# Absolute values and the key factor of a gated linear recurrence: from VectorE to ScalarE

## The chip, the cores and the metric

The kernel runs on one core of one Trainium2 chip. The metric is device time in microseconds (us) of one execution; of several runs the median is given. The engines are TensorE (PE in the profile, PEld for its weight loads), VectorE (DVE), ScalarE (ACT), GpSimd (POOL) and SyncE (SP, which issues the DMAs).

## The reference

One step of a two-layer decoder over 1056 positions: a prompt of 1024 and 8 x 4 sample positions. The first layer is a gated linear recurrence (HGRN2) of 8 heads with a 128x128 state, the second an attention with dilated windows; each has a squared-ReLU MLP. The change lies in the gates of the recurrence:

```python
q, f, i, og = jnp.split((xn @ w_in).astype(jnp.float32), 4, axis=-1)
q = heads(jax.nn.silu(q), A_KDIM)
log_f = heads(jax.nn.log_sigmoid(f) + jnp.log1p(lb * jnp.exp(jnp.minimum(-f, EXP_CLAMP))), A_KDIM)
k = heads((1.0 - lb) * jax.nn.sigmoid(-f), A_KDIM)
v = heads(i, A_VDIM)
...
o = _head_rmsnorm(o, out_gain.reshape(A_HEADS, A_VDIM)) * heads(jax.nn.sigmoid(og), A_VDIM)
```

## The kernel before, in words

`phase_a` (from L326) computes the recurrence. The channels of one head lie on the 128 partitions, the 1056 positions on the free axis, cut into three chunks of 352. For each of the 8 heads four projections of the normed input are made on TensorE (f, q, the value i, and the output gate og of the head before), each as 8 x 3 matmuls per chunk, since every fp32 factor is split into a high and a low part (`mm3`, L185 to L187).

A projected chunk is copied out of PSUM by ScalarE (`ev_to`, L368; for f in `ev_f`, L390). Then the gates follow, chunk by chunk:

- `sigmoid` (L371) is called for q (as silu) and for og. It forms -|x| on VectorE (L376), then exp (L377) and ln(1 + .) (L378) on ScalarE, min(x, 0) minus that on VectorE (L380), exp on ScalarE (L381), and for q a product on VectorE (L383).
- `ev_f` forms -|f| on VectorE (L392), exp (L393) and ln(1 + .) (L394) on ScalarE, the log-sigmoid (L395) and the softplus (L396) on VectorE, the key exp(-softplus) on ScalarE (L397), its factor 1 - lb on VectorE (L398), then the second logarithm (L399 to L402) and the running sum along the positions on VectorE (L404, L408, L412).

The lower bound lb and 1 - lb are made once, from 8 columns (L336 to L341); the tile `e` holds them.

`gla` works the recurrence of one head off, in pieces: it is a generator, and after every half of a projection's chunk (`tick`, called in `mm3` where `fine` is set) the next piece is emitted between the projections' matmuls. One half of a head has seven levels of scores. A level is a subtraction on GpSimd (L536), two exponentials on ScalarE (L539, L540), two products on VectorE (L541, L543), matmuls on TensorE (L554) and a masked copy of their result into the tile `A` on VectorE (L558). Then come the decays (L566 to L573), the transposes of the decayed keys (L618 uses them), four states `S`, one from the other, on VectorE (L626, L628), and matmuls with A and S (L633, L635). The result is normed and gated on VectorE (L640, L647). `gla_sample` does the same for the sample positions.

Each engine works its instructions off in the order of its own queue. That order is fixed when the kernel is built: a planner walks through the program with its own estimates of durations and takes, on each engine, the ready instruction of the highest priority; priority is the order of the program, moved forward where `high_priority` says so (copies out of PSUM by 300, states by 200, levels by 50). A matmul that waits for a PSUM bank, for A or for S holds up every matmul behind it. Of the tiles of the change, `sg` has two buffers and `fn` one.

Of the kernel before, what the change touches and what calls it, by code (L numbers as in the profile page):

```python
# [13 lines left out]
AF = mybir.ActivationFunctionType  # L14
ALU = mybir.AluOpType
# [31 lines left out]
class Kern:  # L47
# [278 lines left out]
    def phase_a(self):  # L326
        nc, tc, a = self.nc, self.tc, self.a
# [7 lines left out]
        e = c.tile([P, 3, KD], F32, name="lbt")  # L335
# [3 lines left out]
        nc.vector.tensor_tensor(e[:, 0], e[:, 0], e[:, 1], op=ALU.mult)  # L339
        nc.vector.tensor_tensor(e[:, 1], e[:, 0], e[:, 0], op=ALU.subtract)  # L340
        nc.vector.tensor_scalar(e[:, 2], e[:, 1], -1.0, 1.0, op0=ALU.mult, op1=ALU.add)  # L341
        self.lb, self.omlb = e[:, 1], e[:, 2]
        ctx = ExitStack()
        s1 = ctx.enter_context(tc.tile_pool(name="gla1", bufs=1, reuse_waits="tile"))
        gp = self.gp = ctx.enter_context(tc.tile_pool(name="gla", bufs=2, reuse_waits="tile"))
# [25 lines left out]
        def sigmoid(x, mul):  # L371

            for c in range(NCH):
                x_ = x[:, c * CW:(c + 1) * CW]
                n = gp.tile([P, CW], F32, name="sg")
                nc.vector.scalar_tensor_tensor(n, x_, -1.0, x_, op0=ALU.mult, op1=ALU.min)  # L376
                nc.scalar.activation(n, n, AF.Exp)  # L377
                nc.scalar.activation(n, n, AF.Ln, bias=1.0)  # L378
                o = n if mul else x_
                nc.vector.scalar_tensor_tensor(o, x_, 0.0, n, op0=ALU.min, op1=ALU.subtract)  # L380
                nc.scalar.activation(o, o, AF.Exp)  # L381
                if mul:
                    nc.vector.tensor_tensor(x_, x_, n, op=ALU.mult)  # L383

        def ev_f(h, b, kt, lf):
            def ev(c, ps):
                sl = slice(c * CW, (c + 1) * CW)
                with hp():
                    f = gp.tile([P, CW], F32, name="fr")
                    nc.scalar.activation(f, ps, AF.Copy)  # L390
                n = gp.tile([P, CW], F32, name="fn", bufs=1)
                nc.vector.scalar_tensor_tensor(n, f, -1.0, f, op0=ALU.mult, op1=ALU.min)  # L392
                nc.scalar.activation(n, n, AF.Exp)  # L393
                nc.scalar.activation(n, n, AF.Ln, bias=1.0)  # L394
                nc.vector.scalar_tensor_tensor(lf[:, sl], f, 0.0, n, op0=ALU.min, op1=ALU.subtract)  # L395
                nc.vector.scalar_tensor_tensor(n, f, 0.0, n, op0=ALU.max, op1=ALU.add)  # L396
                nc.scalar.activation(kt[:, sl], n, AF.Exp, scale=-1.0)  # L397
                nc.vector.tensor_scalar(kt[:, sl], kt[:, sl], self.omlb[:, h:h + 1], None, op0=ALU.mult)  # L398
                nc.vector.tensor_scalar(f, f, -80.0, None, op0=ALU.max)  # L399
                nc.scalar.activation(f, f, AF.Exp, scale=-1.0)  # L400
                nc.scalar.activation(f, f, AF.Ln, scale=self.lb[:, h:h + 1], bias=1.0)
                nc.vector.tensor_tensor(lf[:, sl], lf[:, sl], f, op=ALU.add)  # L402
                n, off = min(CW, NP_ - c * CW), c * CW % P
                nc.vector.tensor_tensor_scan(  # L404
                    b[:, c * CW:c * CW + n], self.reset[:, off:off + n], lf[:, c * CW:c * CW + n],
                    0.0 if c == 0 else b[:, c * CW - 1:c * CW], op0=ALU.mult, op1=ALU.add)
                if n < CW:
                    nc.vector.tensor_tensor_scan(b[:, NP_:], self.reset[:, 448:], lf[:, NP_:], 0.0, op0=ALU.mult, op1=ALU.add)  # L408

                for i in ((), (2, 3), (6, 7))[c]:  # L410
                    s = slice(i * P, i * P + P)
                    nc.vector.scalar_tensor_tensor(b[:, s], lf[:, s], b[:, s.stop - 1:s.stop], b[:, s], op0=ALU.add, op1=ALU.subtract)  # L412
            return ev

        def gate(h, og):
            self.proj(self.wnext(), ops, ev_to(og))
            sigmoid(og, False)
            nc.gpsimd.tensor_copy(self.so[:, h, :], og[:, NP_:])

        self.fine = True  # L420
        for h in range(8):
            b = gp.tile([P, NT], F32, name="b")
            kt = gp.tile([P, NT], F32, name="k")
            q = gp.tile([P, NT], F32, name="q")
            lf = gp.tile([P, NT], F32, name="lf", bufs=1)
            if h == 0:
                w = [self.wnext(), self.wnext()]
                self.proj_n(w, ops, [ev_f(h, b, kt, lf), ev_to(q)])
                for i in range(4):
                    mt = gp.tile([P, 512], F32, name="lv", bufs=6)[:, :480]  # L430
                    nc.sync.dma_start(mt, a["masks"][:, 480 * i:480 * i + 480])
                    nc.vector.tensor_copy(self.masks[:, 480 * i:480 * i + 480], mt)
            else:
                gate(h - 1, og)
                self.proj(self.wnext(), ops, ev_f(h, b, kt, lf))
                self.proj(self.wnext(), ops, ev_to(q))
            sigmoid(q, True)
            vT = gp.tile([P, NT], F32, name="vT", bufs=1)
            self.proj(self.wnext(), ops, ev_to(vT))
            if h % 4 == 0:  # L440
                new = [gp.tile([P, 4, NS], F32, name=f"s_{n}", bufs=1) for n in "bkqv"]
            for d, s in zip(new, (b, kt, q, vT)):
                nc.gpsimd.tensor_copy(d[:, h % 4, :], s[:, NP_:])
            og = gp.tile([P, NT], F32, name="og", bufs=1)
            self.queue.append(self.gla(h, b, kt, q, vT, og))
            if h == 3:
                self.lanes.append(self.gla_sample(0, new))
# [1069 lines left out]
```

## Time and profile before

| | |
|---|---|
| median of 3 runs | 2974.51 us (2974.26 to 2975.25) |
| the profiled execution, its own time | 2977.09 us |
| its span, first to last instruction | 2975.3 us |
| PE busy | 2861.1 us (96%) |
| DVE busy | 1710.7 us (57%) |
| ACT busy | 1301.8 us (44%) |
| POOL busy | 1302.0 us (44%) |

The profile is of one execution. Busy time is summed over the whole span, and so says little of one stage; the rows below are of stretches and lines. "Idle before" is the time in which an engine did nothing just before an instruction, and the releaser is what ended it. The granted clock (PEclk) is the share of TensorE's full speed that the chip allowed in a stretch.

### The profile page before, as it was taken

What the parts mean: (1) busy time and instruction counts of PE and PEld (TensorE: products, weight loads), DVE (VectorE), ACT (ScalarE), POOL (GpSimd) and SP (SyncE); (2) the same over time, 40 slices, a digit from 0 to 9 for tenths busy, and PEclk for the clock granted to TensorE, in tenths of its full rate; (3) what the DMA queues carried; (4) which work ended last, traced back from release to release, by engine and by line L of the source; (5) the groups of instructions that cost most, each with busy time, mean ns of one, the idle gap of its engine ahead of it and who ended that gap; (6) DMA issues with size and microseconds to landing.
All of it is one profiled execution on the core that took longest, in us unless ns stands there. A gap on an engine that the chain in (4) does not pass through costs nothing.

```text
span 2975.3 us, 47214 instructions
## 1 busy us (share of the span) xinstructions
PE 2861.1 (96%) x18144; PEld 2755.7 (93%) x18144; DVE 1710.7 (57%) x3449; ACT 1301.8 (44%) x2972; POOL 1302.0 (44%) x1119
## 2 busy tenths in 40 slices
PE   6999999989999999999899999999999999999999
PEld 5998899979999999999899889889889999999999
DVE  8788788874544444543644565665565445444442
ACT  6666566644333222332435555555545223333221
POOL 5444444551544445544463454433213445444442
PEclk9999999999999999999999999999999999999999
DMA  3111210230111111111212233432551111111112
GB/s 116 34 34 30 71 43 30 69 127 22 47 46 47 47 50 50 46 47 57 93 57 69 80 103 101 133 114 80 189 171 39 47 51 50 43 51 43 50 50 87
DMA packets 131954, 201.90 MB, mean 68 GB/s; under 512 B 26321, under 2 KB 65873, under 8 KB 129681
## 3 DMA queue, kind: packets, MB, share of 16 engines
q1 hardware_dynamic: 131728, 198.88, 21.4%
q8 instruction: 143, 2.34, 0.3%
q14 instruction: 83, 0.67, 0.1%
HBM read 164.04 MB, written 34.80 MB: 67 GB/s over the span
## 4 chain that ended last, share of the span: by engine, by line
PE 57%; POOL 9%; DVE 9%; DMA 6%; issue 6%; ACT 3%; POOLq 0%; SPq 0%; DVEq 0%; ACTq 0%
PE pj L185 10%; PE pj L186 10%; PE pj L187 10%; POOL wlo L132 5%; DMA wraw<-w_dn 4%; PE pj L848 4%; PE pj L849 4%; PE pj L850 4%; POOL wlox L132 2%; PE g L849 2%; PE g L848 2%; PE g L850 2%; PE g L1190 2%; PE g L1162 1%; PE g L1177 1%
## 5 line engine op out<-in xcount | busy, mean ns | idle before, releaser
L185 PE MATMUL pj<-opH,whi 128*128 128x352 f32 (+2 forms) x3408 | 1138.3, 334 | 4.8 <-ACT opH L232 3.5
L186 PE MATMUL pj<-opL,whi 128*128 128x352 f32 (+2 forms) x3408 | 1110.0, 326 | 3.6 <-POOL opL L233 1.9
L187 PE MATMUL pj<-opH,wlo 128*128 128x352 f32 (+2 forms) x3408 | 1106.5, 325 | 2.9 <-POOL wlo L132 2.7
L132 POOL TENSOR_TENSOR wlo<-wraw,whi 128x512 fp32r<-128x512 f32 x404 | 547.6, 1375 | 982.1 <-ACT whi L131 946.6
L185 PEld LDWEIGHTS pj<-opH,whi 128*128 128x128 f32 x3408 | 647.1, 190 | 23.7 <-issue 13.9
L186 PEld LDWEIGHTS pj<-opL,whi 128*128 128x128 f32 x3408 | 648.1, 190 | 14.1 <-issue 5.7
L187 PEld LDWEIGHTS pj<-opH,wlo 128*128 128x128 f32 x3408 | 646.7, 190 | 7.1 <-POOL wlo L132 4.1
L131 ACT ACTIVATE whi<-wraw 128x512 fp32r<-128x512 f32 x404 | 232.7, 622 | 560.7 <-PE g L849 441.8
L762 DVE SCALAR_TENSOR_TENSOR tmp<-pj,scale 128x384 f32<-128x384 f32 (+1 forms) x192 | 100.0, 521 | 303.4 <-PE pj L187 303.4
L862 DVE TENSOR_TENSOR xr<-xr,pj 128x384 f32<-128x384 f32 x336 | 184.5, 553 | 143.7 <-PE pj L850 143.7
L763 ACT ACTIVATE tmp<-tmp 128x384 f32<-128x384 f32 (+1 forms) x192 | 94.8, 494 | 290.5 <-DVE tmp L762 290.2
L536 POOL TENSOR_TENSOR lv<-b 128x512 f32<-128x512 f32 x112 | 127.2, 1148 | 112.3 <-PE g L635 64.7
L132 POOL TENSOR_TENSOR wlox<-wsum,whix 128x512 fp32r<-128x512 f32 x112 | 151.3, 1372 | 0.0
L162 POOL TENSOR_TENSOR wsum<-wraw,wsum 128x256 f32<-128x256 f32 x56 | 41.3, 738 | 170.0 <-DVE wsum L160 167.8
L1167 ACT ACTIVATE pr<-pr,nm 128x128 f32<-128x128 f32 (+1 forms) x192 | 84.1, 440 | 68.8 <-DVE nm L1165 68.8
L211 DVE TENSOR_TENSOR xr<-xr,pj 128x384 f32<-128x384 f32 (+1 forms) x132 | 67.6, 516 | 77.8 <-PE pj L187 39.4
L1164 DVE CUSTOM_DVE_ANT_0 pr<-g,band,rq 128x128 f32<-128x128 f32 (+1 forms) x192 | 68.0, 404 | 77.0 <-PE g L1162 73.2
L148 POOL TENSOR_TENSOR wraw<-wraw,gains 128x512 f32<-128x512 f32 x72 | 89.6, 1250 | 43.9 <-DMA wraw<-w_q 35.1
L768 DVE TENSOR_TENSOR tmp<-tmp 128x384 f32<-128x384 f32 x84 | 79.8, 976 | 46.4 <-ACT tmp L763 46.4
L1014 POOL TENSOR_TENSOR q<-q,cos 32x512 f32<-32x512 f32 x48 | 88.9, 1857 | 30.8 <-DVE rsw L1013 29.5
L1015 DVE TENSOR_TENSOR rsw<-rsw,sin 32x512 f32<-32x512 f32 (+1 forms) x66 | 99.6, 1525 | 0.7
L849 PE MATMUL g<-hL,whi 128*128 128x288 f32 x336 | 99.8, 297 | 0.0
(400 smaller groups left out, 5745.9 us busy)
## 6 DMA issues: line engine op xcount, KB each, us to landing
wraw<-w_up SPq DMA_DIRECT2D x128, 256.0 KB, 2.8
wraw<-w_dn SPq DMA_DIRECT2D x128, 256.0 KB, 2.8
wraw<-w_in SPq DMA_DIRECT2D x64, 256.0 KB, 2.8
wraw<-w_q SPq DMA_DIRECT2D x48, 256.0 KB, 3.0
ub<-us SPq DMA_DIRECT2D x32, 256.0 KB, 2.2
cc<-ck SPq DMA_DIRECT2D x8, 1024.0 KB, 4.9
cc<-cv SPq DMA_DIRECT2D x8, 1024.0 KB, 5.3
wraw<-w_kv SPq DMA_DIRECT2D x24, 256.0 KB, 2.9
```

Of the source, the lines that this page charges most:

```text
L131: nc.scalar.activation(hi[:, j:j + 4, :], raw, AF.Copy)
L132: nc.gpsimd.tensor_tensor(lo[:, j:j + 4, :], raw, hi[:, j:j + 4, :].bitcast(F32), op=ALU.subtract)
L185: nc.tensor.matmul(ps, wh[:, kw, :], xh[:, kx, :], start=(i == 0), stop=False)
L186: nc.tensor.matmul(ps, wh[:, kw, :], xl[:, kx, :], start=False, stop=False)
L187: nc.tensor.matmul(ps, wl[:, kw, :], xh[:, kx, :], start=False, stop=(i == len(ks) - 1))
L536: nc.gpsimd.tensor_tensor(r(lv), r(b), r(b)[:, :, h - 1:h].to_broadcast([P, 256 // h, 2 * h]), op=ALU.subtract)
L762: nc.vector.scalar_tensor_tensor(r, ps, 0.0, self.scale[c], op0=ALU.max, op1=ALU.mult)
L848: nc.tensor.matmul(ps, wh[:, kw, :], xh, start=start and i == 0, stop=False, skip_group_check=True)
L849: nc.tensor.matmul(ps, wh[:, kw, :], xl, start=False, stop=False, skip_group_check=True)
L850: nc.tensor.matmul(ps, wl[:, kw, :], xh, start=False, stop=stop and i == len(items) - 1, skip_group_check=True)
L862: self.nc.vector.tensor_tensor(x(i, c), x(i, c), ps, op=ALU.add)
L1015: nc.vector.tensor_tensor(f(sw), f(sw), sn, op=ALU.mult)
```

## The change

The absolute value is made by ScalarE (function Abs), and the sign goes into the scale of the exponential that follows. The factor 1 - lb of the keys becomes an addend of the exponent: its logarithm is made once, and is given to the exponential of the key as a bias, one value per partition.

```diff
-        self.lb, self.omlb = e[:, 1], e[:, 2]
+        nc.scalar.activation(e[:, 2], e[:, 2], AF.Ln)
+        self.lb, self.lnlb = e[:, 1], e[:, 2]
...
-                nc.vector.scalar_tensor_tensor(n, x_, -1.0, x_, op0=ALU.mult, op1=ALU.min)
-                nc.scalar.activation(n, n, AF.Exp)
+                nc.scalar.activation(n, x_, AF.Abs)
+                nc.scalar.activation(n, n, AF.Exp, scale=-1.0)
...
-                nc.vector.scalar_tensor_tensor(n, f, -1.0, f, op0=ALU.mult, op1=ALU.min)
-                nc.scalar.activation(n, n, AF.Exp)
+                nc.scalar.activation(n, f, AF.Abs)
+                nc.scalar.activation(n, n, AF.Exp, scale=-1.0)
...
-                nc.scalar.activation(kt[:, sl], n, AF.Exp, scale=-1.0)
-                nc.vector.tensor_scalar(kt[:, sl], kt[:, sl], self.omlb[:, h:h + 1], None, op0=ALU.mult)
+                nc.scalar.activation(kt[:, sl], n, AF.Exp, scale=-1.0, bias=self.lnlb[:, h:h + 1])
```

## Rows read from the trace of the kernel before

**Rows 1.** By 75 us: PE, PEld, DVE, ACT, POOL busy; clock; DMA share; GB/s.

```profile
75.00:150.00 75.00, 69.74 (x442) 68.20 (x443) 59.83 (x109) 44.95 (x101) 33.91 (x34) 0.94 0.11 34
...
525.00:600.00 75.00, 68.91 (x448) 66.66 (x446) 66.53 (x122) 48.99 (x119) 37.98 (x37) 0.98 0.26 81
...
675.00:750.00 75.00, 75.00 (x468) 73.72 (x468) 35.97 (x71) 33.15 (x69) 12.91 (x11) 1.00 0.07 22
```

**Rows 2.** TensorE's waits, 75 to 660 us: who waited for whom, total, times, longest.

```profile
PE g L554 <- DVE A L558: 12.2, 7, 2.7
PE g L635 <- DVE S L626: 11.6, 8, 2.3
```

**Rows 3.** VectorE's groups, 0 to 660 us: busy us, mean ns, idle before, releasers.

```profile
L392 DVE SCALAR_TENSOR_TENSOR fn<-fr 128x352 f32<-128x352 f32 x24 | 21.9, 912 | 2.6 <-ACT fr L390 2.6
...
L376 DVE SCALAR_TENSOR_TENSOR sg<-q 128x352 f32<-128x352 f32 x24 | 16.7, 697 | 2.0 <-ACT q L368 1.9
L376 DVE SCALAR_TENSOR_TENSOR sg<-og 128x352 f32<-128x352 f32 x24 | 15.7, 652 | 10.5 <-ACT og L368 10.5
...
L398 DVE TENSOR_SCALAR k<-k,lbt 128x352 f32<-128x352 f32 x24 | 14.2, 592 | 1.4 <-ACT k L397 1.1
```

**Rows 4.** ScalarE's groups, 0 to 660 us, columns as in rows 3.

```profile
L377 ACT ACTIVATE sg<-sg 128x352 f32<-128x352 f32 x48 | 23.7, 495 | 47.7 <-DVE sg L376 47.6
L401 ACT ACTIVATE fr<-fr,lbt 128x352 f32<-128x352 f32 x24 | 14.0, 585 | 0.5
```

**Rows 5.** VectorE in order of time before a wait for S: start, us, instruction.

```profile
167.79 1.32 DVE L392 SCALAR_TENSOR_TENSOR fn<-fr 128x352 f32<-128x352 f32 x1 [0.28 <-ACT fr L390]
...
173.31 0.52 DVE L392 SCALAR_TENSOR_TENSOR fn<-fr 128x352 f32<-128x352 f32 x1
173.74 0.88 DVE L404 TENSOR_TENSOR_SCAN b<-reset,lf 128x352 f32<-128x352 f32 x1
```

**Rows 6.** ScalarE in order of time, the same place.

```profile
169.15 0.50 ACT L393 ACTIVATE fn<-fn 128x352 f32<-128x352 f32 x1 [0.91 <-DVE fn L392]
```

**Rows 7.** VectorE in order of time before a wait for A, a head earlier.

```profile
112.84 1.59 DVE L392 SCALAR_TENSOR_TENSOR fn<-fr 128x352 f32<-128x352 f32 x1
114.36 1.26 DVE L541 TENSOR_TENSOR lv<-lv,q 128x256 f32<-128x256 f32 x1
...
118.32 0.40 DVE L398 TENSOR_SCALAR k<-k,lbt 128x352 f32<-128x352 f32 x1
118.63 0.34 DVE L399 TENSOR_SCALAR fr<-fr 128x352 f32<-128x352 f32 x1
```

**Rows 8.** TensorE in order of time: matmuls that waited, with the wait in brackets.

```profile
72.39 0.90 PE L511 MATMUL g<-ident,vT 128*128 128x128 f32 x3 [4.23 <-ACT vT L368]
...
124.79 0.97 PE L554 MATMUL g<-lv,lk 128*128 128x128 f32 x4 [2.33 <-DVE A L558]
174.87 0.49 PE L635 MATMUL g<-lv,S 128*128 128x128 f32 x2 [1.65 <-DVE S L626]
193.70 0.68 PE L554 MATMUL g<-lv,lk 128*128 128x128 f32 x4 [0.66 <-DVE A L558]
```

**Rows 9.** Busy time by stretches of 15 us, columns as in rows 1.

```profile
105.00:120.00 15.00, 14.15 (x93) 13.57 (x94) 14.72 (x25) 11.02 (x26) 7.80 (x7) 1.00 0.12 37
120.00:135.00 15.00, 12.67 (x76) 12.41 (x75) 13.25 (x29) 8.36 (x18) 3.84 (x7) 0.89 0.10 29
...
195.00:210.00 15.00, 15.00 (x107) 15.00 (x106) 9.03 (x21) 8.89 (x21) 8.18 (x8) 1.00 0.13 42
```

**Rows 10.** ScalarE and VectorE in order of time, the first head.

```profile
38.15 0.19 ACT L337 ACTIVATE lbt<-lbt 128x8 f32<-128x8 f32 x1
...
49.29 0.16 DVE L341 TENSOR_SCALAR lbt<-lbt 128x8 f32<-128x8 f32 x1
...
54.77 1.61 DVE L376 SCALAR_TENSOR_TENSOR sg<-q 128x352 f32<-128x352 f32 x1
```

**Rows 11.** ScalarE's table loads in the whole span, from its groups.

```profile
L78 ACT ACT_TABLE_LOAD x1 | 1.3, 1283 | 0.7 <-PEq L1507 0.7
```

## The prediction

> **What bounds the kernel now.** I read the stretches first. In the recurrence, 75 to 600 us, TensorE is busy for 492.5 of 525 us (seven rows, the first and the last in [rows 1]), so 32.5 us are lost; VectorE runs at 78 to 89% and ScalarE at 59 to 65%. From 675 us on TensorE is busy for 75.00 of 75 and VectorE for 36: TensorE's own queue bounds the rest, and the weights there are far from filling the DMA engines (share 0.07). So the recurrence can only give back what TensorE waits for, and whatever it gives back should arrive at the end whole, since nothing behind it has a time of its own to keep.
>
> Next, who makes TensorE wait. Two waits carry it, both on VectorE: for the masked copy into A, 12.2 us in 7 waits, and for the first state S, 11.6 us in 8, one for each head [rows 2]. The reader is to see that neither producer is dear; both stand late in VectorE's queue.
>
> A second loss is the clock. The granted clock falls to 0.89 in the stretch that begins with the 2.33 us wait at 124.79 [rows 8, 9], a mix of its two levels, 2.4 and 1.2 GHz; 0.11 of 15 us is 1.65 us lost. Over the seven rows of [rows 1] it is 0.94 once and 0.98 six times, so 75 x (0.06 + 6 x 0.02) = 13.5 us. After the short wait of 0.66 us at 193.70 the row stays at 1.00 [rows 8, 9]; the 1.65 us wait at 174.87 is longer, and so near the doubtful middle.
>
> **The change part by part.** *Off VectorE:* L392 (21.9 us), L376 (16.7 + 15.7) and L398 (14.2) [rows 3], 68.5 us of instructions, 72 absolute values and 24 products. Their means of 592 to 912 ns hide a wide spread: one L392 takes 0.52 us, others 1.32 or 1.59 [rows 5, 7], so what one is worth depends on the place.
>
> *Onto ScalarE:* 72 Abs of 128x352. No Abs is in the trace; the nearest row is the exponential of the same tile, 495 ns (L377, [rows 4]), as every ScalarE function of that shape with plain constants lies within some 10 ns of it. That is 35.6 us. The bias of 24 key exponentials is a value per partition; L401, which has such a scale, takes 585 ns against the 495 [rows 4], so 24 x 0.09 = 2.2 us. With one Ln of 8 columns, 38 us go on; an engine at 59 to 65% can hold them. An Abs needs only ScalarE's own copy out of PSUM, so the wait for VectorE ahead of L377, 47.6 us in all [rows 4], and the like ahead of L393, go. That idle time is the cover for the 38 us; where it is absent an Abs costs its 0.5 us to what is queued behind it on ScalarE: copies out of PSUM, the exponentials of the levels, the weight copies.
>
> The Trainium skill speaks against the move: ScalarE: Activation LUTs, Rules for kernel authors, puts max, min and multiplication on VectorE and holds it up to three times faster, in bf16 with one source. By it, as an estimate, an Abs would cost 3 x 0.52 = 1.6 us and the 72 of them 112 us. No run here has bf16 in these lines; in fp32 the rows have 0.495 us against 0.52 at best [rows 5] and 0.65 to 0.91 on average [rows 3, 4], so I go by the rows.
>
> *The wait for S.* Before it VectorE works the first f chunk off [rows 5]. L392 begins at 167.79, and ScalarE's exponential, idle for 0.91 us, begins when it is done, at 169.15 [rows 6]. With Abs on ScalarE, 0.5 of those 0.91 us remain: 0.41 us gained. The second L392, of the next chunk, stands at 173.31 right before the scan at 173.74: 0.43 us. Together 0.84 us of this wait of 1.65. Eight waits give at most 6.7, and one shorter than 0.84 us only itself, so I take 6. What is late next there is ScalarE's chain to L401 and the scan itself (0.88 us).
>
> *The wait for A.* VectorE runs without a gap from 111 us to the wait at 124.79. L392 holds it from 112.84 to 114.36 and L398 from 118.32 to 118.63 [rows 7]: 1.83 us of queue. The exponential behind the absolute value moves too, but ScalarE has level work between, so I take 1.7. The seven waits are 1.74 us each on average [rows 2]; the long ones, as that of 2.33, keep some 0.6, the short ones, as that of 0.66 at 193.70, go whole [rows 8]. If four are long, 12.2 - 4 x 0.7 = 9.4; I take 9, with 0 and 12.2 as ends. Next late: the product of L640 and GpSimd's subtractions.
>
> *The clock.* Waits of 2.33 and 1.65 us become 0.6 and 0.8, near the 0.66 that left the clock at 1.00. If that holds everywhere 13.5 us come back, if the clock goes on falling none. I take 6, nearer to the middle, since rows do not show what a gap of 0.8 us does every time.
>
> *The first head.* TensorE stands 4.23 us at 72.39 for the copy of the value [rows 8], which is queued on ScalarE behind instructions that wait for VectorE. Ahead of it VectorE loses six absolute values and two products, one of them 1.61 us long [rows 10]. Between 0 and the 4.23 us; I take 3.
>
> *The new Ln* waits for VectorE's L341, done at 49.45 [rows 10], and the first biased exponential waits for it. Placed where that exponential is, it costs 0.2 us; queued right behind L337, at 38.15 [rows 10], it would hold ScalarE's splitting of the normed inputs up for 11 us. I take 0: the planner places it after L341 by its own estimate.
>
> *Order.* No DMA is issued or moved. GpSimd's copy of the sample keys now waits for L397 instead of L398, so earlier. The two `sg` buffers make an Abs wait for VectorE's reader two chunks back, long done where ScalarE had been waiting for VectorE. But the planner deals the queues anew, so single places can get worse; with the Abs in front of level exponentials I charge 3 us over the stage (bounds 0 and 0.5 x 24 = 12).
>
> *Sum:* 6 + 9 + 6 + 3 - 3 = 21 us. The profiled execution took 2977.09 us, its span 2975.3, the median of the runs is 2974.51, 2.6 below; the forecast is 2974.5 - 21.5, so **2953 us**.
>
> **The rivals.**
>
> 1. *Everything goes.* With VectorE relieved by 68.5 us every wait on it closes: 12.2 + 11.6, the first head's 4.2 and the clock's 13.5, so 41 us: 2933. For it: VectorE loses 8.6 us of work in each head, twice what TensorE waits there. Against it: the chain of one level still passes four engines.
>
> 2. *The gain is hidden.* The queue is dealt anew so that other VectorE work (L380, L383) takes the freed places before A and S. Then TensorE waits as before: 2971 to 2978. For it: the waits come from order, not from load alone. Against it: these places are in the program's order, which does not change.
>
> 3. *ScalarE takes VectorE's place; slower.* In the stretch before A, the chunk's Abs, one Abs of q and the longer exponential, 0.5 + 0.5 + 0.1 = 1.1 us, come ahead of the decays' exponentials (L567, L570), whose products stand before the copies into A. It decides once they take more than the 1.7 us saved there, so if some four Abs pile up ahead of one level, as when the planner runs q's three chunks early: 2.1 - 1.7 = 0.4 us more on 8 heads, S gains nothing, and on four heads a wait that so far left the clock alone would cost 1.65 us of it: 3 + 7 = 10 us, 2985. Against it: ScalarE's idle time before L377.
>
> 4. *Abs needs another table.* Each Abs between exponentials would then load twice, 72 x 2 x 1.283 us [rows 11] = 185 us: 3160. Against it: copies, squares, exponentials and logarithms alternate throughout with a single load in the span. The Trainium skill (ScalarE: Activation LUTs, Table sets) says that abs is filler in every set; by that this rival falls. No row here has an Abs.
>
> That the change does not do what it says I leave at nothing: the lines go and come as written.
>
> **How the numbers follow.** Forecast with its bounds (2940 to 2966): 0.62. Rival 1: 0.13, so faster 0.75. Hidden: 0.13. ScalarE in the way: 0.10, the table 0.02. Faster or slower means by over 0.2%, 5.9 us, about what a measurement of this kernel can tell from no change. The slowest 0.12 can stay out below; the range reaches down to 2934, nearly all of rival 1, and up to 2973, half of the hidden cases.
>
> **What would show it.** L392, L376 and L398 gone from VectorE; 72 Abs near 0.5 us on ScalarE and one table load; VectorE at 0.7 to 0.75 of the stage; the wait for S near 0.8 us a head, that for A below 1; the 15 us rows at 0.89 mostly at 1.00; the stage shorter by about 21 us and all behind it unchanged. I am wrong if those waits move to another releaser of the same length, if ScalarE's copies out of PSUM release TensorE, or if the clock still falls after gaps below 1 us.

## The result and the profile after

| | before | after |
|---|---|---|
| median of 6 runs each | 2974.88 us (2969.35 to 2977.45) | 2957.82 us (2951.38 to 2964.22) |
| ratio after to before | | 0.9944 [0.9934, 0.9954], so -16.7 us [-19.6, -13.7] |
| the profiled execution (span) | 2977.09 us (2975.3) | 2951.38 us (2949.6) |
| end of the recurrence in it | 728.30 us | 710.12 us |

The change makes the kernel 0.56% faster. "End of the recurrence" is the start of VectorE's first evacuation in the first MLP (L762). I use it for the rest of the document because the code behind it is the same in all kernels and yet varies from execution to execution: it took 2247.0 us before and 2239.5 after, and between 2242.8 and 2249.5 in the kernels of the experiments. Like every row, it is of one execution of each kernel. The profiled execution of after is the shortest of its six, so 7.5 of its 25.7 us lie in code that nobody touched. The recurrence alone gives -18.2 us, which agrees with the ratio.

Line numbers of after between L342 (the new Ln) and L398 are greater by one than before: L377 is the Abs of q and og, L378 and L379 their exponential and logarithm, L393 the Abs of f, L397 the softplus, L398 the biased exponential of the key. From L399 on the numbers agree.

The first row of [rows 1], of after (PE, PEld, DVE, ACT, POOL busy; clock; DMA share; GB/s):

```profile
75.00:150.00 75.00, 72.25 (x478) 70.56 (x478) 55.54 (x104) 50.96 (x115) 35.63 (x35) 0.98 0.13 37
```

Against [rows 1] the first stretch holds 478 matmuls instead of 442, at a clock of 0.98 instead of 0.94. The seven rows of after read 0.98, 1.00, 1.00, 0.98, 1.00, 1.00, 0.98. Over 75 to 600 us VectorE fell from 427.5 to 400.4 us of work (76% of the stretch) while ScalarE rose from 327.8 to 365.9.

TensorE's waits up to 660 us, as in rows 2, show both what went and what came:

```profile
PE g L554 <- ACT sg L378: 6.2, 4, 1.5
PE g L511 <- ACT vT L369: 5.0, 2, 3.7
PE g L635 <- DVE S L626: 4.5, 7, 0.8
PE g L554 <- ACT sg L377: 3.7, 2, 1.9
PE g L554 <- DVE A L558: 2.7, 6, 0.5
PE g L635 <- DVE S L628: 1.5, 2, 0.8
```

The wait for S fell from 11.6 to 4.5 us and the one that is charged to A from 12.2 to 2.7 [rows 2]. But a wait that was not there, 6.2 + 3.7 = 9.9 us in six pieces, is charged to ScalarE's gates of q (L377, L378). The matmuls of one head show where (start, us, wait in brackets):

```profile
168.09 0.49 PE L635 MATMUL g<-lv,S 128*128 128x128 f32 x2 [0.67 <-DVE S L626]
...
185.00 0.68 PE L554 MATMUL g<-lv,lk 128*128 128x128 f32 x4 [0.40 <-DVE A L558]
...
189.15 0.69 PE L554 MATMUL g<-lv,lk 128*128 128x128 f32 x4 [1.55 <-ACT sg L378]
```

The first masked copy after S now costs 0.40 us, and the next one, 4 us later, costs 1.55. ScalarE's groups of after have the prices of what was added (busy us, mean ns, idle before):

```profile
L378 ACT ACTIVATE sg<-sg 128x352 f32<-128x352 f32 x48 | 23.6, 491 | 0.9
L398 ACT ACTIVATE k<-fn,lbt 128x352 f32<-128x352 f32 x24 | 14.1, 589 | 31.2 <-DVE fn L397 31.2
L393 ACT ACTIVATE fn<-fr 128x352 f32<-128x352 f32 x24 | 11.9, 496 | 0.4
L377 ACT ACTIVATE sg<-q 128x352 f32<-128x352 f32 x24 | 11.8, 492 | 0.4
L78 ACT ACT_TABLE_LOAD x1 | 1.3, 1283 | 0.7 <-PEq L1507 0.7
```

An Abs costs 492 to 496 ns, the biased exponential 589, and there is one table load as in [rows 11]. The 47.7 us of idle time ahead of the exponential of the gates [rows 4] shrank to 0.9.

### The profile page after: what moved, and what is told of

Same layout as the page of the kernel before. It is cut to its first block, busy times and chain, and to the rows that moved or that the text cites. A ratio compares the mean times of both kernels' runs of the same rounds, so it can differ in the third digit from the quotient of the medians.

```text
span 2949.6 us, 47181 instructions
## 1 busy us (share of the span) xinstructions
PE 2851.9 (97%) x18144; PEld 2746.8 (93%) x18144; DVE 1661.5 (56%) x3353; ACT 1332.1 (45%) x3045; POOL 1311.5 (44%) x1119
## 4 chain that ended last, share of the span: by engine, by line
PE 58%; POOL 10%; DVE 7%; DMA 6%; issue 5%; ACT 4%; POOLq 0%; DVEq 0%; SPq 0%; ACTq 0%
PE pj L185 11%; PE pj L186 10%; PE pj L187 10%; POOL wlo L132 5%; PE pj L848 4%; DMA wraw<-w_dn 4%; PE pj L849 4%; PE pj L850 4%; POOL wlox L132 2%; PE g L849 2%; PE g L848 2%; PE g L850 2%; PE g L1190 2%; PE g L1162 2%; PE g L1177 1%
## 5 line engine op out<-in xcount | busy, mean ns | idle before, releaser
L186 PEld LDWEIGHTS pj<-opL,whi 128*128 128x128 f32 x3408 | 645.8, 189 | 11.5 <-issue 5.7
L762 DVE SCALAR_TENSOR_TENSOR tmp<-pj,scale 128x384 f32<-128x384 f32 (+1 forms) x192 | 99.9, 520 | 303.0 <-PE pj L187 303.0
L1167 ACT ACTIVATE pr<-pr,nm 128x128 f32<-128x128 f32 (+1 forms) x192 | 84.1, 439 | 67.7 <-DVE nm L1165 67.5
L848 PE MATMUL g<-hH,whi 128*128 128x288 f32 x336 | 98.9, 294 | 0.0
```

What stands on the lines that cost most here:

```text
L186: nc.tensor.matmul(ps, wh[:, kw, :], xl[:, kx, :], start=False, stop=False)
L762: nc.vector.scalar_tensor_tensor(r, ps, 0.0, self.scale[c], op0=ALU.max, op1=ALU.mult)
L848: nc.tensor.matmul(ps, wh[:, kw, :], xh, start=start and i == 0, stop=False, skip_group_check=True)
```

## The new wait, followed back

A matmul into `g` does not read `sg`; the name in the bracket is only the semaphore event nearest to the end. The rows of VectorE below have the two masked copies (L558): the first ends at 184.43 + 0.43 = 184.86 and TensorE goes on at 185.00, the second ends at 189.00 and TensorE goes on at 189.15. So this wait, too, is for L558, which is late, and with it the wait for A is 2.7 + 9.9 = 12.6 us in all, not less than the 12.2 of before. What stood ahead of it, on GpSimd, ScalarE and VectorE of after in order of time:

```profile
182.17 2.41 POOL L443 COPY s_k<-k 128x32 f32<-128x32 f32 x1 [2.79 <-ACT k L398]
184.54 1.04 POOL L566 TENSOR_TENSOR lv<-b 128x512 f32<-128x512 f32 x1
...
187.74 0.19 POOL L572 COPY ebl<-lv 128x4 f32<-128x4 f32 x1 [0.98 <-ACT lv L570]
```

```profile
185.61 0.63 ACT L567 ACTIVATE lv<-lv 128x512 f32<-128x512 f32 x1 [1.90 <-POOL lv L566]
186.15 0.48 ACT L378 ACTIVATE sg<-sg 128x352 f32<-128x352 f32 x1
186.66 0.50 ACT L379 ACTIVATE sg<-sg 128x352 f32<-128x352 f32 x1
187.06 0.61 ACT L570 ACTIVATE lv<-b 128x512 f32<-128x512 f32 x1
```

```profile
181.99 0.74 DVE L640 SCALAR_TENSOR_TENSOR kdT<-kdT,gains,rstd 128x512 f32<-128x512 f32 x1
182.65 0.42 DVE L543 TENSOR_TENSOR lk<-lv,k 128x256 f32<-128x256 f32 x1
182.98 0.76 DVE L647 TENSOR_TENSOR xr<-kdT,og 128x256 f32<-128x256 f32 x2
183.66 0.42 DVE L541 TENSOR_TENSOR lv<-lv,q 128x256 f32<-128x256 f32 x1
183.99 0.52 DVE L402 TENSOR_TENSOR lf<-lf,fr 128x352 f32<-128x352 f32 x1
184.43 0.43 DVE L558 COPY_PREDICATED A<-masks,g 128x256 f32<-128x256 uint8 x1
184.76 1.49 DVE L404 TENSOR_TENSOR_SCAN b<-reset,b,lf 128x320 f32<-128x320 f32 x1
...
187.13 0.68 DVE L568 TENSOR_TENSOR lv<-lv,k 128x512 f32<-128x512 f32 x1
187.96 0.69 DVE L573 TENSOR_TENSOR lv<-lv,q 128x512 f32<-128x512 f32 x1
188.57 0.43 DVE L558 COPY_PREDICATED A<-masks,g 128x256 f32<-128x256 uint8 x1
```

Read it from the top. GpSimd's copy of 32 sample keys (L443), which was let through in 0.26 us before, takes 2.41 us: it lasts through L543, L647, L541 and L402, each with two inputs in SBUF, and ends 0.15 us into a masked copy, whose input `g` is in PSUM. The decays' subtraction (L566) is queued behind it in both kernels, and starts 16.4 us after the matmul that waited for S (184.54 - 168.09), where before it was 13.0 (187.91, in the fence below, less the 174.87 of [rows 8]); the exponential L567 waits 1.90 us for it, q's L378 and L379 follow on ScalarE ahead of the second exponential L570, and the product L573, which stands ahead of the masked copy on VectorE, waits for GpSimd's L572 behind L570. GpSimd of before in order of time at the same place, and the group of the copy there (busy us, mean ns, idle before):

```profile
187.69 0.26 POOL L443 COPY s_k<-k 128x32 f32<-128x32 f32 x1 [1.71 <-DVE k L398]
187.91 1.22 POOL L566 TENSOR_TENSOR lv<-b 128x512 f32<-128x512 f32 x1
...
L443 POOL COPY s_k<-k 128x32 f32<-128x32 f32 x8 | 2.2, 279 | 14.4 <-DVE k L398 14.4
```

and the same group of after:

```profile
L443 POOL COPY s_k<-k 128x32 f32<-128x32 f32 x8 | 15.2, 1898 | 16.7 <-PE pj L187 11.2 <-ACT k L398 5.6
```

That chain holds VectorE up by little, though. Between the two masked copies, from 184.43 to 188.57, lie 4.14 us, and VectorE works through them: the scan L404, L408, L543, two L412 and the two products. Only 0.15 us ahead of L573 are idle (187.13 + 0.68 = 187.81 to 187.96). Besides that the scan takes 1.49 us, while the late subtraction L566 runs on GpSimd, and 0.87 before, where nothing runs there. The rest of the wait is order. VectorE of before at the same place:

```profile
191.04 0.87 DVE L404 TENSOR_TENSOR_SCAN b<-reset,b,lf 128x320 f32<-128x320 f32 x1
...
193.13 0.42 DVE L558 COPY_PREDICATED A<-masks,g 128x256 f32<-128x256 uint8 x1
...
194.67 0.43 DVE L558 COPY_PREDICATED A<-masks,g 128x256 f32<-128x256 uint8 x1
```

There the scan and what follows it stand ahead of the first masked copy, in after behind it. So the first comes 16.66 us after the copy of S instead of 18.59 (184.43 - 167.77 and 193.13 - 174.54), and the second 4.14 us after the first instead of 1.54. What the first gained and what the second lost are two sides of one exchange in VectorE's queue. The scan itself does not come earlier: 16.99 us after the copy of S in after, 16.50 before, for VectorE, with less to do, now stands idle for 2.01 us at 173.04, waiting for ScalarE's logarithm L401.

Six of the eight key copies of after take 2.41 us, at the same place of six heads. The Trainium skill (SBUF — State Buffer, SBUF: two separate sides) says that VectorE and GpSimd share a pair of ports, which one instruction holds as a lock, with the loser blocked outright; a VectorE instruction with two SBUF inputs takes it against a GpSimd one that reads SBUF. The rows agree in kind: 2.41 us beside such instructions, 0.26 beside L399, which has one input.

## The experiments

Each was timed in alternation with the kernel before. "End" is the end of the recurrence in one profiled execution; "head" is the time from one head's copy of S on VectorE to the next one's, in the second head (and the third, where it differs).

| kernel | ratio to before [95%] | end, us | head, us |
|---|---|---|---|
| before | 1 | 728.3 | 69.0, 67.4 |
| after | 0.9944 [0.9934, 0.9954] | 710.1 | 66.2 |
| e1_f | 0.9992 [0.9983, 1.0002] | 722.0 | 66.5, 68.1 |
| e2_sig | 0.9993 [0.9984, 1.0002] | 724.8 | 68.7, 67.2 |
| e3_key | 0.9983 [0.9974, 0.9991] | 720.9 | 66.6 |
| e4_noabs | 0.9883 [0.9868, 0.9898] | 694.4 | 64.2 |
| e5_side | 0.9910 [0.9896, 0.9925] | 698.1 | 63.8 |
| e6_qvec | 1.0007 [0.9997, 1.0016] | 728.4 | 68.9 |
| e7_dec20 | 0.9925 [0.9909, 0.9942] | 706.3 | 64.8 |
| e8_bdec | 1.0006 [0.9996, 1.0016] | 732.8 | 69.0, 67.5 |
| e9_q_scopy | 0.9966 [0.9954, 0.9979] | 719.8 | 66.4, 68.0 |
| e10_fkey | 1.0012 [1.0002, 1.0022] | 733.9 | 69.2 |
| e11_scopy | 0.9928 [0.9916, 0.9940] | 707.8 | 65.6 |
| e12_scopy_dec | 0.9914 [0.9901, 0.9928] | 702.1 | 64.7 |

### The parts alone

**e1_f**, the kernel before with the edit of `ev_f`'s absolute value alone.

```diff
-                nc.vector.scalar_tensor_tensor(n, f, -1.0, f, op0=ALU.mult, op1=ALU.min)
-                nc.scalar.activation(n, n, AF.Exp)
+                nc.scalar.activation(n, f, AF.Abs)
+                nc.scalar.activation(n, n, AF.Exp, scale=-1.0)
```

> Only the absolute value of f goes to ScalarE (L392); those of q and og and the factor of the keys stay on VectorE. The whole change moved the end of the recurrence forward by 18.2 us (first MLP evacuation 728.3 to 710.1) and the median by 17. Theory of place: what counts is what stood in VectorE's queue right ahead of the copies into A and of S, and that was above all L392; then most of it comes already here: 11 to 15 us, the wait for S falls from 11.6 to 4 to 6 us, that for A from 12.2 to below 5. Theory of load: what counts is VectorE's time in the stage, 21.9 of 68.5 us, so 18 x 0.32 = 6 us, with both waits shortened by about a third.

Measured 0.9992, -2.4 us, an interval that includes no change, and less than either theory. TensorE's waits, then VectorE ahead of the wait for A at 123.95:

```profile
PE g L554 <- DVE A L558: 15.5, 7, 2.8
PE g L635 <- DVE S L626: 6.7, 7, 1.5
```

```profile
111.67 1.51 DVE L543 TENSOR_TENSOR lk<-lv,k 128x256 f32<-128x256 f32 x1
...
115.82 1.26 DVE L543 TENSOR_TENSOR lk<-lv,k 128x256 f32<-128x256 f32 x1
117.00 1.36 DVE L396 SCALAR_TENSOR_TENSOR fn<-fr,fn 128x352 f32<-128x352 f32 x1
```

S gains 4.9 us and A loses 3.3 [rows 2]. L392 of 1.59 us is gone from that place [rows 7], but four instructions of 1.26 to 1.51 us stand there, and an L543 that took 0.41 us before (at 117.99) is one of them: VectorE needs 18.56 us from the copy of S to that masked copy, 18.69 before. Here the long durations belong to the place, and pass to the instruction that stands there. So the 1.5 us that the prediction read off L392 was not L392's own, and what S gains is handed on to A, where TensorE arrives earlier.

**e2_sig**, the same edit in `sigmoid` alone (q and og).

> Only the absolute values of q and og go to ScalarE (L376, 32.4 us of VectorE's time); f and the factor of the keys stay on VectorE. Theory of place: these stand behind the waits for A and S in VectorE's queue, except in the first head and behind the last projection: 2 to 4 us less, the waits for S and A near 11 and 12 us as before. Theory of load: 18 x 32.4 / 68.5 = 8.5 us less, both waits about half as long. ScalarE in the way: q's exponentials ahead of the decays' (L570) make the wait for A longer than before, so no gain or up to 5 us more.

Measured 0.9993, an interval that includes no change, with waits of 15.4 for A and 8.0 for S. A is longer, as the third case had it, but not for its reason: VectorE is at the masked copy 18.7 us after S, as before. It is the exchange of e1.

**e3_key**, the logarithm and the bias alone.

```diff
+        nc.scalar.activation(e[:, 2], e[:, 2], AF.Ln)
...
-                nc.scalar.activation(kt[:, sl], n, AF.Exp, scale=-1.0)
-                nc.vector.tensor_scalar(kt[:, sl], kt[:, sl], self.omlb[:, h:h + 1], None, op0=ALU.mult)
+                nc.scalar.activation(kt[:, sl], n, AF.Exp, scale=-1.0, bias=self.lnlb[:, h:h + 1])
```

> Only the factor of the keys goes into the bias of the exponential (L398 gone, 14.2 us of VectorE's time; the Ln of 8 columns is there); all absolute values stay on VectorE. Theory of place: 0.31 us of the 1.83 us ahead of the wait for A, nothing ahead of that for S, where VectorE waits for ScalarE anyway: 1 to 3 us less. Theory of load: 18 x 14.2 / 68.5 = 3.7 us less. If the longer key exponential or the Ln were in the way: 1 to 3 us more.

Measured 0.9983, -5.1 us, a little more than either theory. The waits of TensorE:

```profile
PE g L635 <- DVE S L626: 10.8, 8, 2.4
PE g L554 <- POOL ebl L572: 4.5, 4, 1.2
PE g L554 <- DVE A L558: 3.7, 5, 1.2
```

It is the part that relieves A: 17.54 us from S to the first masked copy, 12.2 down to 3.7 + 4.5 (the wait named after L572 is at the same matmuls). Again it is order: the scan starts 16.63 us after S, no earlier than before, but the two L412 and an L543 now stand behind the first masked copy. The smallest of the prices on VectorE in [rows 3] gave the most, though the three intervals overlap.

**e10_fkey**, after with `sigmoid` as before: the absolute value of f and the key factor together. **e6_qvec**, after with only q's absolute value back on VectorE:

```diff
-                nc.scalar.activation(n, x_, AF.Abs)
-                nc.scalar.activation(n, n, AF.Exp, scale=-1.0)
+                if mul:
+                    nc.vector.scalar_tensor_tensor(n, x_, -1.0, x_, op0=ALU.mult, op1=ALU.min)
+                else:
+                    nc.scalar.activation(n, x_, AF.Abs)
+                nc.scalar.activation(n, n, AF.Exp, scale=1.0 if mul else -1.0)
```

> The absolute value of f and the factor of the keys on ScalarE, q and og on VectorE: the two parts that alone gave 4 and 5 us, without the third that gave 2. If the parts add up, 9 us less than before, 66 us from head to head, clock at 0.99. If the long copy of the keys on GpSimd comes back with f's Abs (it has 1.2 us on average with f alone, 0.34 with the keys alone, 1.6 in e6_qvec), the result is like e6_qvec's, within 4 us of before, with a copy above 1.5 us and a wait for A above 15 us in all.

> The changed kernel with q's absolute value alone back on VectorE (24 of the 72; 16.7 us of VectorE's time before). In the changed kernel the second masked copy into A of a half stands in VectorE's queue behind the product of the decays (L573), which waits for GpSimd's copy of the exponential L570, and that stands on ScalarE behind q's exponential and logarithm (two instructions, 1.0 us); TensorE waits 1.55 us there in each head. If q's instructions ahead of L570 cause it, that wait falls to about 0.5 us and the time is 4 to 8 us below the changed kernel. If VectorE's load counts, it is 3 to 5 us above it. If it is the place of the products in VectorE's queue whatever ScalarE does, within 2 us of it.

Measured 1.0012 and 1.0007. Two parts of which each alone is no loss are a loss of 3.6 us together, and putting back 24 of the 96 instructions that left VectorE takes the whole gain, which none of the three cases named for e6 had. Of e6, the waits, and in order of time ScalarE and VectorE:

```profile
PE g L557 <- DVE A L561: 19.5, 6, 3.5
```

```profile
189.03 0.63 ACT L570 ACTIVATE lv<-lv 128x512 f32<-128x512 f32 x1 [2.33 <-POOL lv L569]
189.56 0.57 ACT L404 ACTIVATE fr<-fr,lbt 128x352 f32<-128x352 f32 x1
```

```profile
190.17 0.53 DVE L405 TENSOR_TENSOR lf<-lf,fr 128x352 f32<-128x352 f32 x1 [1.89 <-ACT fr L404]
```

(Lines stand three lower here.) The copy of the sample keys starts at 186.02 and takes 1.98 us; the decays' subtraction follows it, their exponential waits 2.33 us, and now the second logarithm of f is queued behind that on ScalarE. VectorE stands idle for 1.89 us, and the masked copy behind it makes TensorE wait 3.12 us at 194.14. The clock over 75 to 600 us stays at 0.97, as before. e10 shows the same two waits, 2.33 and 1.89 us. In after the same product (L402) is done at 184.51, before L567 has its input, so VectorE has nothing to wait for there: the order that the planner made with q's Abs on ScalarE is the better one. In e1, e2 and e3 the scan stands ahead of the first masked copy, as before; in e6, e10 and after it stands behind.

### The ceiling, and what ScalarE's load costs

**e4_noabs**, after with the absolute values left out. **e5_side**, e4 with each Abs written into a tile that nobody reads.

```diff
-                nc.scalar.activation(n, x_, AF.Abs)
-                nc.scalar.activation(n, n, AF.Exp, scale=-1.0)
+                nc.scalar.activation(n, x_, AF.Exp, scale=-1.0)
```

```diff
+                nc.scalar.activation(gp.tile([P, CW], F32, name="dm", bufs=1), x_, AF.Abs)
                 nc.scalar.activation(n, x_, AF.Exp, scale=-1.0)
```

> The changed kernel with the absolute values left out (the exponential is of -x itself), so VectorE is relieved as there and ScalarE has 72 instructions less. If ScalarE's 36 us of Abs lie in its idle time, the time is that of the changed kernel, within 2 us. If they stand ahead of the decays' exponential (L570), which is what the new waits of 9.9 us charged to q's exponentials would then be, those waits shrink by an Abs or two in each head and the time is 4 to 10 us below the changed kernel, 22 to 27 below the kernel before.

> The kernel without absolute values (e4_noabs, 2940 us, 17 below the changed kernel) plus the 72 Abs again, each at its old place on ScalarE but into a tile of its own that nobody reads; the exponential is of -x itself, so the values are not the reference's. If ScalarE's added time (36 us) is what the changed kernel loses against e4_noabs, this one takes as long as the changed kernel, 2955 to 2960. If it is the longer chain (copy, Abs, exp, ln one after the other), this one stays near e4_noabs, 2940 to 2943. The rows: the copy of S of one head to the next is 66.2 us in the changed kernel and 64.2 in e4_noabs.

Measured 0.9883 and 0.9910: e4 lies further below after than expected, and e5 between its two cases. The wait for A of e4 (1.3 us more stand under another name):

```profile
PE g L552 <- DVE A L556: 3.6, 5, 1.5
```

The Abs cost after 710.1 - 694.4 = 15.7 us in all. Of these e5, which does the same work on ScalarE, keeps 698.1 - 694.4 = 3.7 (by the ratios to before it is 8.0 us of 18.1): the first copy of S comes 2.7 us later than in e4, the stretch with the sample positions takes 83.5 instead of 79.2 us, and the steady heads (63.8 us) are no longer than e4's (64.2). So in a steady head the Abs cost ScalarE's queue next to nothing, as predicted. The other 12 us, 66.2 - 63.8 = 2.4 us a head, come with the dependence of the exponential on the Abs, but hardly by a longer chain: Abs and exponential of f start 0.53 us apart in after (166.75 and 167.28) and 0.40 in e5 (166.21 and 166.61). Without the dependence the planner deals another order. ScalarE runs the second chunk's L401 ahead of two instructions on the output (L656, L657) that stand ahead of it in after, VectorE waits for it 1.19 us instead of 2.01, and the first masked copy comes 12.88 us after S. The key copy is short in e4 and e5 (354 and 346 ns on average). What each of these is worth, and whether ScalarE's load would show in the order of after, the runs do not show.

### The new wait

Two edits take its parts away one by one: the products of the decays that stand ahead of the second masked copy, and the long key copy on GpSimd.

**e7_dec20**, after with the decays' priority lowered; **e8_bdec**, the same on the kernel before.

```diff
-                with self.tc.high_priority(offset=50):
+                with self.tc.high_priority(offset=50 if i % 8 < 7 else -20):
```

> The changed kernel with the decays (L566 to L573) no longer moved forward by 50 but back by 20, so that in VectorE's queue one or two more masked copies into A come ahead of their products; all else is as in the changed kernel. If the wait of 1.55 us a head charged to q's exponentials is really the masked copy behind L573, it goes: 8 to 12 us below the changed kernel, 2946 to 2950, and 64.7 us from head to head instead of 66.2. If it is ScalarE that TensorE waits for, the time stays within 2 us of the changed kernel. If the decayed keys (L618) come late for it, a new wait on kdT and 3 to 8 us more.

> The kernel before with the same move of the decays back by 20; gates and keys as before. There the wait for A (2.33 us) is at the first masked copy of a half, which stands ahead of the decays' products, so the move should give little: 0 to 4 us less than before. If it gives as much as in the changed kernel (8 to 12 us), the products of the decays were as much in the way before the change, and the place of the absolute values has nothing to do with it.

e7: 0.9925, 3.8 us earlier at the end of the recurrence than after, a head of 64.8 instead of 66.2 us: 1.4 of the 1.55 us. The first head (+1.2 us), the stretch with the sample positions (+1.5) and what follows the last head (+2.3) give part of it back, so half of what was expected arrives. In the third head the second masked copy follows the first after 2.71 us instead of 4.14. The key copy is as long as ever (1904 ns) and the scan still takes 1.50, so their length alone does no harm. The waits left:

```profile
PE g L635 <- DVE S L626: 4.0, 6, 0.8
PE g L554 <- DVE A L558: 2.8, 6, 0.5
```

e8: 1.0006, no gain. In before the wait is at the first masked copy, ahead of which no decays stand (A 13.9, S 11.5). The same edit is worth nothing in one kernel and some 4 us in the other.

**e11_scopy**, after with the four copies of samples (L443) on ScalarE; **e9_q_scopy**, the same on e6; **e12_scopy_dec**, e11 with e7's edit.

```diff
-                nc.gpsimd.tensor_copy(d[:, h % 4, :], s[:, NP_:])
+                nc.scalar.activation(d[:, h % 4, :], s[:, NP_:], AF.Copy)
```

> The changed kernel with the four copies of the sample columns (L443) on ScalarE instead of GpSimd. In the changed kernel the copy of the keys takes 2.4 us on GpSimd where it took 0.26 before, and the decays' subtraction waits behind it; from there the wait of 1.55 us a head on the second masked copy into A follows. If so, that wait goes or falls below 0.5 us, the period from 66.2 to 64.7 us, and the time is 8 to 12 us below the changed kernel, 2946 to 2950. If ScalarE's queue is what holds the decays up, four more copies there make it 0 to 4 us longer than the changed kernel.

> The kernel with q's absolute value back on VectorE (e6_qvec, no gain against before, 68.9 us from head to head, a wait for A of 3.1 us in each) with one more edit: the four copies of the sample columns of a head (L443) go from GpSimd to ScalarE. In e6_qvec GpSimd's copy of the keys takes 2.4 us instead of 0.26, its subtraction for the decays waits behind it, and on ScalarE the second logarithm of f stands behind the decays' exponential. If that copy is the cause, the wait for A falls below 1.5 us, the period to 65 to 67 us, and the time to 2952 to 2960, 15 to 22 below before. If q's absolute value on VectorE costs by its load, or by its place in VectorE's queue, the period stays above 68 us and the time within 5 us of before.

> The changed kernel with both edits: the sample copies on ScalarE, and the decays moved back by 20 as in e7_dec20 (2953, 64.8 us from head to head). If both edits take away the same wait, the time is that of the better of the two, within 3 us. If the move of the decays works by VectorE's queue and the copies by GpSimd's, they add up to 2942 to 2947, with a period near 64 us, that of the kernel without absolute values.

e11: 0.9928, short of the 8 to 12 us expected. Its matmul at the place of the 1.55 us, its wait in all, and the scan:

```profile
190.22 0.69 PE L554 MATMUL g<-lv,lk 128*128 128x128 f32 x4 [0.69 <-DVE A L558]
...
PE g L554 <- DVE A L558: 9.1, 12, 1.1
...
186.69 0.87 DVE L404 TENSOR_TENSOR_SCAN b<-reset,b,lf 128x320 f32<-128x320 f32 x1
```

Of 0.40 + 1.55 us a head 0.71 + 0.69 remain. GpSimd's subtraction is done before the scan, the scan takes 0.87 us again, the 0.15 us of idle time ahead of L573 are gone, and the second masked copy follows the first after 3.28 us (186.36 and 189.64): the move of the copy takes away 0.86 of the 1.55 us. The first masked copy costs 0.31 more, so a head is 0.6 us shorter. e9: 0.9966, 8.5 us earlier than e6, with this wait for A:

```profile
PE g L557 <- DVE A L561: 10.2, 5, 2.5
PE g L557 <- POOL sebl L528: 5.2, 2, 2.6
```

The two waits under the second name (257.95 and 547.87 us) are for the same masked copy as the others, so 19.5 us became 15.4, and 3.12 us a head became 2.46, where less than 1.5 was expected. VectorE's idle time of 1.89 us is gone, so the copy was a cause there; but the scan stands ahead of the first masked copy again, which comes 18.65 us after S, as before, and e9 stays 9.7 us behind after. What else q's absolute value sets in order I have not told apart. e12: 0.9914, 2952.23 us, the lowest ratio of the kernels that compute everything: 25.6 us under before, 8.0 us ahead of after at the end of the recurrence. Each of e7's and e11's intervals overlaps after's; e12's does not.

## Why the prediction came out right, and the step that did not

Forecast 2953 us (its sum is 21 us, it takes off 21.5), measured 2957.8, inside the range; faster, as forecast. By its steps:

| step | forecast | measured | from |
|---|---|---|---|
| wait for S | -6 | -6.0 | 11.6 to 4.5, but L628's from 0.4 to 1.5 |
| wait for A, first masked copy | -9 | -9.5 | 12.2 to 2.7 |
| clock | -6 | -9 | 13.5 to 75 x 3 x 0.02 = 4.5 |
| first head | -3 | -2.5 | first L554 at 78.7 instead of 81.1 |
| ScalarE's charge | +3 | +9.9 | second masked copy, waits charged to L377, L378 |
| sum | -21 | -17.1 | the end of the recurrence: -18.2; ratio: -16.7 |

The first row of [rows 1] begins at 75 us, so some of the first head's gain is in the clock's too; that the sum comes so near the measurement is in part luck.

**S** was right in size and reason: seven waits of 0.64 us on average, 0.8 at most, and the exponential follows ScalarE's own Abs.

**A** was right in size only, and only for the first masked copy; that is luck. The working (1.52 us of L392 and 0.31 of L398) took the duration of an instruction for what its removal is worth. e1 shows that L392's 1.5 us stay when it goes, since other instructions take them over, and in e3, where only L398 goes, A gains by order. Relief of VectorE's load did not bring its queue forward: the scan starts 16.50 us after S before and 16.47 to 16.99 in e1, e2, e3 and after. The 1.9 us a head came because the scan, the two L412 and what lies between them went behind the first masked copy, and the second paid for it. Taken together, A gave back nothing (12.2 to 12.6).

**ScalarE's charge**, which was to hold what the queues, dealt anew, make worse, is the term that was mis-sized: 9.9 us, inside its bounds of 0 and 12 but three times the value taken. Its mechanism was not the one of the working either. In a steady head of e5 the 72 Abs cost next to nothing. What costs is the order on VectorE: scan, L412 and products ahead of the second masked copy. A sentence under *Order* failed with it: "GpSimd's copy of the sample keys now waits for L397 instead of L398, so earlier". It was priced at nothing. The copy did not come earlier but later after S, 14.1 us behind the waiting matmul (182.17 - 168.09) instead of 12.8 (187.69 against the 174.87 of [rows 8]), and lasted 2.41 us instead of 0.26, so the decays behind it started 3.4 us late. That is worth 0.86 of the 1.55 us (e11), through the longer scan above all. Rival 3 named the products ahead of the copy into A, which e7 confirms, but held ScalarE to be what makes them late; L573 waits for that 0.15 us. At 1.65 us in each of six waits the new wait took as much as the first masked copy had gained. e7 takes it away, e11 about half of it.

**The clock** gave more than I took, 9 us, and so made up for A. My doubt was what gaps near 1.6 us do. In after, the row that holds the waits of 0.40 and 1.55 us stays at 1.00, where [rows 9] have 0.89 after 2.33:

```profile
180.00:195.00 15.00, 13.05 (x87) 12.53 (x86) 13.49 (x31) 11.24 (x25) 6.66 (x6) 1.00 0.07 20
```

What is left of the loss lies in the stretches with the longest gaps, 3.0 to 3.7 us (first head, sample positions, the decayed keys of the last head).

**The Ln** cost nothing: it runs at 49.28 us for 0.19 us, right behind L341 and ahead of the first biased exponential. **The table** (rival 4) is out: one load. The Trainium skill's line that abs is filler in every set (ScalarE: Activation LUTs, Table sets) agrees. The Trainium skill's rule that VectorE is up to three times faster in bf16 (ScalarE: Activation LUTs, Rules for kernel authors) would have made an Abs 1.6 us by the prediction's estimate, and the rows, in fp32, have 0.49. **Rival 1** (everything goes) fails at the new wait, but e4, which leaves the absolute values out, shows with 34.8 us that most of its size is there to be had without them. **Rival 2** (the gain is hidden) is what happened to the parts: e1 and e2 each shorten S and lengthen A. What was held against it, that these places are in the program's order, which does not change, does not hold in after, where the first masked copy and the scan changed places.

Of the signs named in advance, three were off: VectorE stands at 0.76 of the stage, not 0.70 to 0.75; a wait below 1 us for A holds for the first masked copy only; and another releaser did appear, in name, for a wait as long in all as the one that went.

## What to carry to other kernels

An instruction that is long at one place and short at another need not take its length along when it is moved: look whether its neighbours are long too, and expect the next one to inherit it. When work leaves an engine, look which of its instructions change places in the queue before counting what the lost ones took: here a masked copy went ahead of the scan and the next one stayed behind it, and the new wait of 9.9 us was as much as the change had won on A; one line of priority removed it. Follow the small instructions on other engines too: a copy of 32 columns that came at another moment made up about half of that wait. Parts of a change in a planned order do not add up: alone these gave -2, -2 and -5 us, two of them together +4, all three -17.

## What the runs showed of the hardware

A GpSimd copy of 128x32 takes 0.26 us at one place and 2.41 us, nearly ten times as long, at another. While it was held, VectorE went through L640, L543, L647, L541 and L402 without a gap. Why it was not let in between two of these, yet got through beside L399 before, the runs do not show.

In e1 a head in which the clock row falls is 1.6 us longer than one in which it does not: 68.1 and 66.5 us. The second and third heads of before differ as much, 69.0 and 67.4 us, but with clocks of 0.98 and 0.97 (105.53 to 174.54 and 174.54 to 241.90 us): each has one fall. The row of 0.89 at 120 to 135 us is behind the second head's wait for A; the one at 165 to 180 is ahead of the third's, which then is 0.66 instead of 2.33 us [rows 8]. There the time lost to the clock is for the most part time that TensorE would have waited. In e1's second head, whose longest gap is the 2.38 us at 123.95, the rows from 105 to 165 us all stay at 1.00, while before a gap of 2.33 us was followed by 0.89 [rows 8, 9]. So no gap length read here separates the two by itself.

A Ln, an Abs and an exponential with constants take the same 0.49 us on ScalarE in this shape; a bias per partition adds 0.10 (589 against 491 ns). That every function of the shape lies within 10 ns, as the prediction says, holds where the input is in SBUF; the copies out of PSUM (L368, L390) take 446 to 454 ns.
